# Key and value projections moved between the blocks of the recurrence, y carried through DRAM, and two pairs of 256-column projections done 512 columns at a time

## The chip, the cores and the metric

The kernel runs on one core of a Trainium2 chip. The metric is device microseconds from the first to the last instruction of that core. The engines that matter here are PE (TensorE, matmuls), DVE (VectorE), ACT (ScalarE), POOL (GpSimd) and SP, which issues all DMAs of this kernel from one queue, in its program's order.

## The reference

One decoder layer with T = 512 tokens and D = 1024 channels, in fp32. Two token mixers read the same normalized x: a gated linear recurrence over 1344 channels in 4 blocks, and sparse attention of 16 heads in 4 groups. Their outputs are merged by sigmoid gates, and a squared-ReLU MLP of width 4096 follows. The part that matters:

```python
xn = rmsnorm(x, norm_mix)
(u_rnn, u_gate, q, k_c, v_c, k_s, v_s, k_w, v_w, g_nsa, g_a, g_b) = jnp.split(xn @ w_in, cuts, axis=-1)
h_a = rg_lru(causal_depthwise_conv(u_rnn, conv_w, conv_b), gate_a_w, gate_a_b, gate_x_w, gate_x_b, lru_lambda)
y_a = h_a * jax.nn.gelu(u_gate, approximate=True)
y_b = nsa_mixer(q, k_c, v_c, k_s, v_s, k_w, v_w, g_nsa, rel_bias, ...)
merged = jax.nn.sigmoid(g_a) * (y_a @ proj_a) + jax.nn.sigmoid(g_b) * (y_b @ proj_b)
h = x + merged @ w_out
z = rmsnorm(h, norm_mlp) @ w_mlp_in
return h + jnp.square(jax.nn.relu(z)) @ w_mlp_out
```

`rg_lru` multiplies each block of 336 channels with two gate matrices and runs h[t] = a[t] h[t-1] + u[t] over the tokens. `k_s, v_s` and `k_w, v_w` are the keys and values (256 columns each) of the selected and of the window branch; `k_c, v_c` those of the compressed branch, which pass through a small MLP (phi) first.

## The kernel before

Every fp32 product is made of two parts. A weight tile `wraw` (2 buffers of 2048 elements a partition) comes by DMA; POOL rounds 1024 elements of it into `wh` (line 133) and DVE takes the rest into `wl` (line 134), each with 2 buffers. `mm3` (lines 138 to 140) then issues three matmuls: high by high, high by low, low by high. x is held as `XH` and `XL` in the same way, with channels on the partitions and 512 tokens behind them.

The work is written in this order. First x is normalized and transposed. Then `u_tiles` makes the column tiles of u, 128 columns each (tiles `mm`, 3 PSUM buffers, 24 matmuls of 512 tokens); `Cols` loads their weights in pairs and prepares the next tile's one ahead. Its sink puts the causal convolution into `uc`: one operation on ACT and three taps on DVE (line 326, 511, 510 and 509 elements), after which the PSUM buffer is free; or, for the tiles of the gate branch, gelu into `gg`. DMAs of SP repack `uc` into tiles `ub` of 112 channels for the blocks. `lru(b)` is one block of the recurrence: `ub` is split into `uh` and `ul`, 54 matmuls of 112 x 512 with the gate weights `gwh` and `gwl` follow (tiles `lru`, 4 PSUM buffers), and then a chain on ACT, POOL and DVE up to the scans on DVE (line 379). The result `rr` is repacked by DMAs into `hy`, and `y_tile(t)` multiplies it with `gg` on DVE and splits it at once into `YH` (POOL, line 390) and `YL` (DVE, line 391). The program's order is: tiles 0 to 5 of u, block 0, tiles 6 to 9, y, block 1, tiles 10 to 13, y, block 2, tiles 14 to 18, y, block 3, tiles 19 and 20, y.

Then come the token-major projections, `tok_cols`: KS, VS, KW (256 columns), VW (304, with the branch gates) and the queries of group 0 (256). The weights move and x stands still; four token tiles fill the four `lru` buffers, and a sink norms the heads of each (`head_norm`, tiles `sq` and `hrs`) or splits the values into `VV`. Then `ZW` makes the compressed keys and values as four column tiles like those of u (tiles `mm`, with their sinks `zdk` and `zdv`), phi follows, and with it, as filler of PE, the projection of y (`proj_a`, tiles `mf`, from `YH` and `YL`). In attention, a list of units of scores (tiles `sc`, line 850) and products with the values (`po`, line 888) is interleaved with more filler: the queries of groups 1 to 3 and the merge gates. `bias_copies` copies a row of the table of position biases to 128 partitions in DRAM, and `EC` takes nine small DMAs from a table.

Each engine runs its own instructions in a fixed order; the framework fixes it when the kernel is built, from a timeline that it works out, in which the splits of weights carry a raised priority of 300 (`PRIO`).

Of the kernel before, what the change touches and what calls it, by code (L numbers as in the profile page):

```python
# [68 lines left out]
def layer(ctx, tc, x, norm_mix, w_in, conv_w, conv_b, gate_a_w, gate_a_b, gate_x_w, gate_x_b,  # L69
# [22 lines left out]
    ya_es = ExitStack()  # L92
    yap = ya_es.enter_context(pool("ya", "right"))
    YH = yap.tile([128, NY, T], F32R, name="YH")
    YL = yap.tile([128, NY, T], F32R, name="YL")
    for t in (YH, YL):
        G.memset(f32(t[0:64, 0]), 0.0)
# [384 lines left out]
    kn = kv.tile([128, 4, 4, 2, 64], F32, name="kn")  # L482
    VV = kv.tile([128, 4, 2, 4, 128], F32R, name="VV")
    # the last token tile first
    gates = kv.tile([128, 4, 48], F32, name="gates")
    KC = kv.tile([128, 4, 2, 32], F32R, name="KC")
    QN = {0: kv.tile([128, 4, 256], F32, name="qn")}
    VC = kv.tile([128, 4, 2, 128], F32R, name="VC")
    G.memset(f32(VC), 0.0)

    def rstd_heads(sq, nh, name, pl):
        ss = pl.tile([128, nh], F32, name=name, bufs=2)
        V.tensor_reduce(ss, sq, axis=AX, op=OP.add)
        V.tensor_scalar(ss, ss, 1.0 / 64, EPS, op0=OP.mult, op1=OP.add)
        G.tensor_tensor(ss, ss, halfs[:, :nh], op=OP.pow)
        return ss
# [5 lines left out]
    # columns of w_in with the tokens on the partitions, four token tiles at once  # L502
    def tok_cols(c0, n, sink):
        step = WH // n
        pss = [psr.tile([128, T], F32, name="lru", bufs=4) for _ in range(4)]
        per = 8 if 8 * n <= WR else 4
        for k0 in [k for c in range(0, 8, per) for k in range(c, c + per, step)]:
            if k0 % per == 0:
                v = raw(128, per, n, (None, rows(win, c0, n)[:, k0:k0 + per]))
            kr = k0 % per  # L510
            k1 = min(kr + step, per) - kr + k0
            wh, wl = split(v[:, kr:kr + k1 - k0], k1 - k0, n)
            for i in range(4):
                ts = slice(128 * i, 128 * i + 128)
                for k in range(k0, k1):
                    mm3(pss[i][:, :n], XH[:, k, ts], XL[:, k, ts], wh[:, k - k0], wl[:, k - k0], k == 0, k == 7)
        for i in range(4):
            sink(i, pss[i])

    def head_norm(d4, ps, pl):  # L520
        sq = pl.tile([128, 4, 64], F32, name="sq", bufs=2)
        src = ps[:, :256].rearrange("p (h d) -> p h d", d=64)
        S.activation(d4, src, AF.Copy)
        S.activation(sq, src, AF.Square)
        rs = rstd_heads(sq, 4, "hrs", pl)
        V.tensor_tensor(d4, d4, rs.unsqueeze(2).to_broadcast([128, 4, 64]), op=OP.mult)

    def k_sink(br):
        def sink(i, ps):
            head_norm(kn[:, i, :, br], ps, kvp)  # L530
        return sink

    def v_sink(br):
        def sink(i, ps):
            src = ps[:, :256].rearrange("p (g d) -> p g d", d=64)
            S.activation(VV[:, i, br, :, 0:64], src, AF.Copy)
            V.tensor_tensor(VV[:, i, br, :, 64:128], src, f32(VV[:, i, br, :, 0:64]), op=OP.subtract)
            if br == 1:
                S.activation(gates[:, 3 - i], ps[:, 256:304], AF.Tanh, scale=0.5)
                V.tensor_scalar(gates[:, 3 - i], gates[:, 3 - i], 0.5, 0.5, op0=OP.mult, op1=OP.add)  # L540
                if i == 0:
                    gc = gates[:, 3].rearrange("p (h c) -> p h c", c=3)[:, :, 0]
                    # rows before the first whole block see no compressed key
                    G.affine_select(gc, gc, pattern=[[0, 16]], compare_op=OP.is_ge, fill=0.0,
                                    base=-31, channel_multiplier=1)
        return sink

    def q_sink(i, ps):
        head_norm(QN[0][:, i].rearrange("p (h d) -> p h d", d=64), ps, kvp)
# [59 lines left out]
    with pool("kvp") as kvp:  # L609
        tok_cols(COL_KS, 256, k_sink(0))  # L610
        tok_cols(COL_VS, 256, v_sink(0))
        tok_cols(COL_KW, 256, k_sink(1))
        tok_cols(COL_VW, 304, v_sink(1))
        for h in range(BC):
            bias_copies(h)
        tok_cols(COL_Q, 256, q_sink)
    with pool("ph") as ph:
# [569 lines left out]
```

## Time and profile before

| what | value |
|---|---|
| runs (median of 3) | 1084.92 us (1084.01 to 1088.92) |
| span of the profiled execution | 1088.0 us, mean granted clock 0.988 |
| PE busy | 1047.6 us (96%), 5405 matmuls |
| DVE busy | 669.0 us (61%) |
| POOL busy | 374.5 us (34%) |
| ACT busy | 348.1 us (32%) |
| DMA | 128.41 MB, mean 118 GB/s |

Shares of busy time are averages over the whole span. The time of the profiled execution is its span, 1088.0 us; it lies within the runs, at their upper end. "Granted clock" is the share of full speed at which TensorE was run; 1.00 is 2.4 GHz and 0.50 is 1.2 GHz.

### The profile page before, as it was taken

How to read it: one execution, taken by the hardware profiler on the slowest of the kernel's cores; microseconds unless marked ns; L12 is line 12 of the kernel's file. 1: busy time of each engine (PE TensorE's matmuls, PEld its weight loads, DVE VectorE, ACT ScalarE, POOL GpSimd, SP SyncE). 2: the span in 40 equal slices, each digit the busy share in tenths (PEclk: the TensorE clock that was granted, in tenths of full speed). 3: DMA queues.
4: the chain of work that ended last, by engine and by line, in shares of the span. 5: the costliest groups of instructions: out<-in, count | busy, mean ns of one | idle time of the engine just before them, and what ended most of it. 6: DMA issues, size and time to landing. Idle time of an engine off the chain costs nothing.

```text
span 1088.0 us, 14783 instructions
## 1 busy us (share of the span) xinstructions
PE 1047.6 (96%) x5405; PEld 885.4 (81%) x5405; DVE 669.0 (61%) x1225; ACT 348.1 (32%) x754; POOL 374.5 (34%) x411
## 2 busy tenths in 40 slices
PE   6999899999999999999999999899999999999998
PEld 5767677899778798988988877788888888888886
DVE  5589989954664597778778677554333334444443
ACT  4143353512332375756757611032111111111110
POOL 4243435444231274545646533201111121111110
PEclk9999899999999899999999999999999999999999
DMA  7635323433454633424333267521323233232322
GB/s 176 148 102 168 98 84 96 114 122 107 104 152 149 184 98 120 145 80 119 98 122 107 78 213 256 206 70 41 115 80 114 79 115 116 78 117 78 116 78 78
DMA packets 110199, 128.41 MB, mean 118 GB/s; under 512 B 23119, under 2 KB 87407, under 8 KB 110127
## 3 DMA queue, kind: packets, MB, share of 16 engines
q1 hardware_dynamic: 110127, 127.47, 38.9%
q8 instruction: 43, 0.70, 0.3%
q14 instruction: 29, 0.24, 0.1%
HBM read 109.45 MB, written 15.64 MB: 115 GB/s over the span
## 4 chain that ended last, share of the span: by engine, by line
PE 76%; DVE 9%; DMA 5%; issue 5%; POOL 2%; SPq 1%; ACT 1%; DVEq 0%; POOLq 0%; ACTq 0%
PE mf L138 5%; PE am L140 5%; PE am L139 5%; PE am L138 5%; PE mf L140 5%; PE mf L139 5%; PE mi L140 5%; PE mi L138 5%; PE mi L139 5%; PE sc L850 4%; PE po L888 4%; PE pt L869 3%; PE lru L139 2%; PE lru L140 2%; DVE wl L134 2%
## 5 line engine op out<-in xcount | busy, mean ns | idle before, releaser
L133 POOL TENSOR_SCALAR wh<-wraw 128x1024 fp32r<-128x1024 f32 (+2 forms) x115 | 127.0, 1108 | 260.9 <-PE mi L139 119.3
L134 DVE TENSOR_TENSOR wl<-wraw,wh 128x1024 fp32r<-128x1024 f32 (+2 forms) x115 | 141.7, 1235 | 42.0 <-POOL wh L133 37.5
L861 POOL TENSOR_SCALAR pp<-pp,sm,gates 128x512 f32<-128x512 f32 (+3 forms) x128 | 93.1, 735 | 71.3 <-DVE sm L859 58.4
L140 PE MATMUL am<-mwh,zl 128*128 128x512 f32 x256 | 99.3, 389 | 0.0
L139 PE MATMUL am<-mwl,zh 128*128 128x512 f32 x256 | 99.3, 389 | 0.0
L138 PE MATMUL am<-mwh,zh 128*128 128x512 f32 x256 | 98.8, 389 | 0.0
L140 PE MATMUL mi<-XH,wl 128*128 128x512 f32 x240 | 93.5, 390 | 0.3 <-DVE wl L134 0.3
L138 PE MATMUL mi<-XH,wh 128*128 128x512 f32 x240 | 93.4, 389 | 0.1
L139 PE MATMUL mi<-XL,wh 128*128 128x512 f32 x240 | 93.4, 389 | 0.0
L1130 DVE TENSOR_TENSOR zl<-Z,zh 128x512 fp32r<-128x512 f32 x32 | 36.3, 1136 | 88.4 <-ACT zh L1129 88.4
L140 PE MATMUL mm<-XH,wl 128*128 128x512 f32 (+1 forms) x216 | 83.5, 388 | 6.5 <-DVE wl L134 6.5
L138 PE MATMUL mm<-XH,wh 128*128 128x512 f32 (+1 forms) x216 | 83.4, 388 | 1.0 <-DVE uc L326 0.5
L139 PE MATMUL mm<-XL,wh 128*128 128x512 f32 (+1 forms) x216 | 83.0, 385 | 1.0 <-DVE XL L217 1.0
L133 POOL TENSOR_SCALAR mwh<-wraw 128x1024 fp32r<-128x1024 f32 x32 | 33.9, 1060 | 138.5 <-PE am L140 131.4
L1103 DVE SCALAR_TENSOR_TENSOR Z<-mi,zr 128x512 f32<-128x512 f32 x30 | 20.7, 691 | 97.3 <-ACT zr L1102 97.3
L858 ACT ACTIVATE pp<-pp,mx 128x512 f32<-128x512 f32 (+3 forms) x128 | 71.5, 560 | 27.9 <-DVE mx L856 24.8
L856 DVE CUSTOM_DVE_ANT_0 pp<-sc,BT 128x512 f32<-128x512 f32 (+3 forms) x128 | 59.1, 484 | 23.4 <-PE sc L850 11.0
L1129 ACT ACTIVATE zh<-Z 128x512 fp32r<-128x512 f32 x32 | 20.2, 632 | 136.5 <-PE am L139 134.4
L1102 ACT ACTIVATE zr<-mi 128x512 f32<-128x512 f32 x30 | 18.0, 600 | 141.7 <-PE mi L140 136.9
L875 ACT ACTIVATE PH<-pt 128x512 fp32r<-128x512 f32 (+1 forms) x96 | 49.2, 524 | 36.7 <-PE pt L869 35.9
L850 PE MATMUL sc<-KK,QS 128*128 128x512 f32 (+3 forms) x256 | 58.2, 334 | 2.5 <-DMA KK<-KK 2.5
L876 DVE TENSOR_TENSOR PL<-pt,PH 128x512 fp32r<-128x512 f32 (+1 forms) x96 | 55.8, 591 | 3.9 <-ACT PH L875 3.6
(258 smaller groups left out, 2683.6 us busy)
## 6 DMA issues: line engine op xcount, KB each, us to landing
wraw<-in_w_in_dram SPq DMA_DIRECT2D x26, 1024.0 KB, 5.4
wraw<-in_w_mlp_in_dram SPq DMA_DIRECT2D x16, 1024.0 KB, 5.5
wraw<-in_w_mlp_out_dram SPq DMA_DIRECT2D x16, 1024.0 KB, 4.8
tab_p<-tab_t SPq DMA_DIRECT2D x16, 320.0 KB, 5.4
wraw<-in_proj_a_dram SPq DMA_DIRECT2D x8, 640.0 KB, 6.1
BT<-tab_p SPq DMA_DIRECT2D x16, 256.0 KB, 3.5
wraw<-in_proj_b_dram SPq DMA_DIRECT2D x4, 1024.0 KB, 5.5
wraw<-in_w_out_dram SPq DMA_DIRECT2D x4, 1024.0 KB, 5.7
```

The source lines that it names most:

```text
L133: G.tensor_scalar(h, v, 1.0, 0.0, op0=OP.mult, op1=OP.add)
L134: V.tensor_tensor(l, v, f32(h), op=OP.subtract)
L138: PE.matmul(ps, lh, rh, start=start, stop=False)
L139: PE.matmul(ps, lh, rl, start=False, stop=False)
L140: PE.matmul(ps, ll, rh, start=False, stop=stop)
L850: ins = PE.matmul(ps[:, cs], grp.Q[r][:, ts], grp.K[br][:, hl, :128 * (i + 1)], start=hl == 0, stop=hl == 1)
L856: V.tensor_tensor_reduce(out=pp[:, cs], in0=ps[:, cs], in1=BTS[h][:, 384 - 128 * i:], scale=1.0, scalar=3e38, op0=OP.add, op1=OP.min, accu ...
L858: S.activation(pp[:, cs], pp[:, cs], AF.Exp, bias=mx, scale=-1.0, accum_out=sm)
L861: G.tensor_scalar(pp[:, cs], pp[:, cs], sm, gt, op0=OP.mult, op1=OP.mult)
L875: S.activation(ph, pv, AF.Copy)
L876: V.tensor_tensor(pl, pv, f32(ph), op=OP.subtract)
L888: PE.matmul(po[:, 128 * kt:], VV[:, kt, br, g], P[n][:, KT0[kt]:KT0[kt] + 128 * (4 - kt)], start=False, stop=br == 1 and kt == 3 and n == 1)
```

## The change

`tok_cols` moves up into the recurrence. KS and VS become one projection of 512 columns ahead of block 0; KW (256) comes ahead of block 1, behind tiles 6 to 9 of u; VW (304) ahead of block 2, behind tiles 10 to 13. The queries of groups 0 and 1 become one projection of 512 columns behind the recurrence, and the filler of group 1 in attention goes. Keys, values and queries get their memory before the recurrence; `YH` and `YL` get theirs after it. So `y_tile` writes y to DRAM (`y_d`), and `y_back` reads it (`yr`, 6 buffers) and splits it, two tiles ahead of the query projection and three in each of its steps. Every third column tile of u has buffers of its own for its split (`xwh`, `xwl`). `bias_copies` moves behind the queries.

```diff
         def prep(self, n, prio=PRIO):
             if n < len(self.starts) and n not in self.got:
-                self.got[n] = split(self.load(n), 8, 128, prio=prio)
+                own = {}
+                if self.third is not None and n % 3 == 2:
+                    own = {"pl": self.third, "tags": ("xwh", "xwl"), "bufs": 1}
+                self.got[n] = split(self.load(n), 8, 128, prio=prio, **own)
...
+    def s_sink(i, ps):
+        k_sink(0)(i, ps)
+        v_sink(0, 256)(i, ps)
+
+    def q_sink(i, ps):
+        for g in range(2):
+            head_norm(QN[g][:, i].rearrange("p (h d) -> p h d", d=64), ps, kvp, 256 * g)
...
         V.scalar_tensor_tensor(y, GG[t][p:], 0.5, y, op0=OP.mult, op1=OP.mult)
-        G.tensor_scalar(YH[p:, t], y, 1.0, 0.0, op0=OP.mult, op1=OP.add)
-        V.tensor_tensor(YL[p:, t], y, f32(YH[p:, t]), op=OP.subtract)
+        SP.dma_start(y_d[p:, t], y)
...
+    UW.third = rn
     for n in range(2):
         u_sink(UO[n])(p2[n])
     u_tiles(2, 2 + GT)
...
+    tok_cols(COL_KS, 512, s_sink)
     lru(0)
...
     u_tiles(6, 10)
+    tok_cols(COL_KW, 256, k_sink(1))
     for t in (1, 2):
         y_tile(t)
     lru(1)
     u_tiles(10, 14)
+    tok_cols(COL_VW, 304, v_sink(1))
...
+    def y_back(t):
+        p = 64 if t == 0 else 0
+        y = kvp.tile([128, T], F32, name="yr", bufs=6)[p:]
+        SP.dma_start(y, y_d[p:, t])
+        G.tensor_scalar(YH[p:, t], y, 1.0, 0.0, op0=OP.mult, op1=OP.add)
+        V.tensor_tensor(YL[p:, t], y, f32(YH[p:, t]), op=OP.subtract)
...
-    with pool("kvp") as kvp:
-        tok_cols(COL_KS, 256, k_sink(0))
-        tok_cols(COL_VS, 256, v_sink(0))
-        tok_cols(COL_KW, 256, k_sink(1))
-        tok_cols(COL_VW, 304, v_sink(1))
-        for h in range(BC):
-            bias_copies(h)
-        tok_cols(COL_Q, 256, q_sink)
+    back = iter([1, 2, 3, 4, 5, 6, 7, 8, 9, 10, 0])
+
+    def some_back(n):
+        for _, t in zip(range(n), back):
+            y_back(t)
+
+    with pool("kvq") as kvp:
+        some_back(2)
+        tok_cols(COL_Q, 512, q_sink, lambda: some_back(3))
+    for h in range(BC):
+        bias_copies(h)
...
-    work = 16 * 5.2 + 3 * 10.4 - TAIL
-    add_q(1)
+    work = 16 * 5.2 + 2 * 10.4 - TAIL
```

The order of DVE near the program's start, from behind the normalized rows of x to the fifth tile of u. Before (`uc_359` and `uc_367` are the first two tiles of u, out of PSUM tiles `mm_106` and `mm_107`, `uc_407` the third; `wl_375`, `wl_379` and `wl_422` are the weights of the third, fourth and fifth tile):

```order
L326 SCALAR_TENSOR_TENSOR uc_359<-mm_106,cw_310,uc_359 128x511
L134 TENSOR_TENSOR wl_375<-wraw_284,wh_374 128x1024
L326 SCALAR_TENSOR_TENSOR uc_359<-mm_106,cw_310,uc_359 128x510
L326 SCALAR_TENSOR_TENSOR uc_367<-mm_107,cw_310,uc_367 128x511
L134 TENSOR_TENSOR wl_379<-wraw_284,wh_378 128x1024
L326 SCALAR_TENSOR_TENSOR uc_359<-mm_106,cw_310,uc_359 128x509
L326 SCALAR_TENSOR_TENSOR uc_367<-mm_107,cw_310,uc_367 128x510
L326 SCALAR_TENSOR_TENSOR uc_367<-mm_107,cw_310,uc_367 128x509
L326 SCALAR_TENSOR_TENSOR uc_407<-mm_382,cw_310,uc_407 128x511
L134 TENSOR_TENSOR wl_422<-wraw_419,wh_421 128x1024
```


and now (`uc_364`, `uc_372` and `uc_412` are the same three tiles of u, `mm_99` and `mm_100` the PSUM tiles, `xwl_380`, `wl_384` and `wl_427` the weights of the third, fourth and fifth tile):

```order
L128 TENSOR_TENSOR xwl_380<-wraw_277,xwh_379 128x1024
L398 SCALAR_TENSOR_TENSOR uc_364<-mm_99,cw_303,uc_364 128x511
L128 TENSOR_TENSOR wl_384<-wraw_277,wh_383 128x1024
L398 SCALAR_TENSOR_TENSOR uc_364<-mm_99,cw_303,uc_364 128x510
L398 SCALAR_TENSOR_TENSOR uc_372<-mm_100,cw_303,uc_372 128x511
L128 TENSOR_TENSOR wl_427<-wraw_424,wh_426 128x1024
L398 SCALAR_TENSOR_TENSOR uc_364<-mm_99,cw_303,uc_364 128x509
L398 SCALAR_TENSOR_TENSOR uc_372<-mm_100,cw_303,uc_372 128x510
L398 SCALAR_TENSOR_TENSOR uc_372<-mm_100,cw_303,uc_372 128x509
L398 SCALAR_TENSOR_TENSOR uc_412<-mm_387,cw_303,uc_412 128x511
```


The weights of the fifth tile, `wl_427`, moved ahead of the last tap of the first tile (509 elements), the two last taps of the second and the first of the third.

The order of SP at the end of the recurrence. Before, from the repacking of the last block to the third key and value load behind it (`rr_1475` is the last block's result):

```order
L384 DMA hy_1572<-rr_1475 16x512
L384 DMA hy_1572<-rr_1475 112x512
L121 DMA wraw_1943<-in_w_in_dram 128x8x256
L480 DMA EC_1659<-tab_c_350 15x16x56
L480 DMA EC_1659<-tab_c_350 16x16x56 x7
L480 DMA EC_1659<-tab_c_350 1x16x56
L121 DMA wraw_2085<-in_w_in_dram 128x4x304
L121 DMA wraw_2143<-in_w_in_dram 128x4x304
```


and now, from the second of the three last writes of y, which follow the same repacking (`yr` are the reads, `wraw_2393` the weights of the third and fourth compressed column tile):

```order
L462 DMA y_d_349<-hy_2004 128x512
L462 DMA y_d_349<-hy_2009 128x512
L555 DMA EC_2093<-tab_c_343 15x16x56
L555 DMA EC_2093<-tab_c_343 16x16x56 x7
L555 DMA EC_2093<-tab_c_343 1x16x56
L571 DMA yr_2116<-y_d_349 128x512
L571 DMA yr_2120<-y_d_349 128x512
L571 DMA yr_2158<-y_d_349 128x512
L571 DMA yr_2162<-y_d_349 128x512
L571 DMA yr_2166<-y_d_349 128x512
L571 DMA yr_2198<-y_d_349 128x512
L115 DMA wraw_2393<-in_w_in_dram 128x8x256
```


The writes of y and its first six reads moved in, with the nine `EC` between them, ahead of `wraw_2393`; the loads of keys and values are gone from here.

The order of DVE behind the queries, up to the weights of the second compressed column tile. Before (`hrs` and `qn` belong to the norm of the queries, `wl_2377` are those weights):

```order
L493 TENSOR_REDUCE hrs_2342<-sq_2339 128x4
L494 TENSOR_SCALAR hrs_2342<-hrs_2342 128x4
L526 TENSOR_TENSOR qn_1673<-qn_1673,hrs_2334 128x256
L493 TENSOR_REDUCE hrs_2350<-sq_2347 128x4
L526 TENSOR_TENSOR qn_1673<-qn_1673,hrs_2342 128x256
L494 TENSOR_SCALAR hrs_2350<-hrs_2350 128x4
L493 TENSOR_REDUCE hrs_2358<-sq_2355 128x4
L134 TENSOR_TENSOR wl_2377<-wraw_2370,wh_2376 128x1024
```


and now (`wl_2361` are those weights, `YL_2110` is the low part of y, split from what was read back):

```order
L573 TENSOR_TENSOR YL_2110<-yr_2116,YH_2109 128x512
L339 TENSOR_TENSOR qn_356<-qn_356,hrs_2283 128x256
L309 TENSOR_REDUCE hrs_2299<-sq_2296 128x4
L339 TENSOR_TENSOR qn_357<-qn_357,hrs_2291 128x256
L310 TENSOR_SCALAR hrs_2299<-hrs_2299 128x4
L309 TENSOR_REDUCE hrs_2307<-sq_2304 128x4
L573 TENSOR_TENSOR YL_2110<-yr_2120,YH_2109 128x512
L310 TENSOR_SCALAR hrs_2307<-hrs_2307 128x4
L573 TENSOR_TENSOR YL_2110<-yr_2158,YH_2109 128x512
L128 TENSOR_TENSOR wl_2361<-wraw_2354,wh_2360 128x1024
```


Three splits of y, each of which needs a read of y, moved in ahead of the weights.

## Rows read from the trace of the kernel before

**Rows 1.** Windows of PE by stage: us, PE busy (instructions), clock, DMA share, GB/s.
```profile
29.80:54.50 24.70, 22.94 (x98) 1.00 0.67 164
54.50:194.30 139.80, 131.89 (x549) 0.98 0.39 113
194.30:290.70 96.40, 91.74 (x610) 0.98 0.42 116
290.70:380.00 89.30, 83.86 (x416) 0.96 0.50 148
```

**Rows 2.** Waits of PE in the recurrence: total us, times, longest us.
```profile
PE mm L140 <- DVE wl L134: 3.0, 1, 3.0
PE lru L140 <- DVE gwl L134: 2.5, 2, 1.3
```

**Rows 3.** Windows of PE: three idle stretches, each with the stretch behind it.
```profile
118.00:122.20 4.20, 1.06 (x4) 0.84 0.42 109
120.80:127.60 6.80, 5.37 (x13) 0.50 0.02 5
281.20:284.00 2.80, 0.50 (x3) 1.00 0.68 168
284.70:288.10 3.40, 3.40 (x10) 0.50 0.88 249
363.00:365.80 2.80, 0.36 (x2) 1.00 0.93 251
366.60:373.40 6.80, 6.80 (x22) 0.50 1.04 350
```

**Rows 4.** Windows of PE: 256-column matmuls alone, then 512-column matmuls alone.
```profile
210.00:237.00 27.00, 27.00 (x227) 1.00 0.50 143
1000.00:1050.00 50.00, 50.00 (x223) 1.00 0.25 85
```

**Rows 5.** Timeline of 28 to 50 us: start, duration, engine, line, operation [idle before].
```profile
32.88 2.18 DVE L326 SCALAR_TENSOR_TENSOR uc<-mm,cw,uc 128x509 f32<-128x509 f32 x3
...
33.01 1.60 SPq L121 DMA_DIRECT2D wraw<-in_w_in_dram  x2
...
35.67 0.39 PE L138 MATMUL mm<-XH,wh 128*128 128x512 f32 x1
...
39.25 1.05 POOL L133 TENSOR_SCALAR wh<-wraw 128x1024 fp32r<-128x1024 f32 x1 [7.82 <-DMA wraw<-in_w_in_dram]
...
40.34 1.23 DVE L134 TENSOR_TENSOR wl<-wraw,wh 128x1024 fp32r<-128x1024 f32 x1 [2.90 <-POOL wh L133]
...
41.48 0.74 DVE L326 SCALAR_TENSOR_TENSOR uc<-mm,cw,uc 128x510 f32<-128x510 f32 x1
```

**Rows 6.** Timeline: the last gate matmul of the recurrence.
```profile
194.05 0.40 PE L140 MATMUL lru<-uh,gwl 112*112 112x512 f32 x1
```

**Rows 7.** Timeline of 203 to 217 us: end of the recurrence.
```profile
204.21 3.44 DVE L379 TENSOR_TENSOR_SCAN rr<-ee,ii 112x512 f32<-112x512 f32 x3
...
209.83 6.80 SPq L480 DMA_DIRECT2D EC<-tab_c  x9
...
212.59 1.10 DVE L389 SCALAR_TENSOR_TENSOR hy<-gg,hy 128x512 f32<-128x512 f32 x1
```

**Rows 8.** The page's costliest groups: total busy us, mean ns of one.
```profile
L133 POOL TENSOR_SCALAR wh<-wraw 128x1024 fp32r<-128x1024 f32 (+2 forms) x115 | 127.0, 1108 | 260.9 <-PE mi L139 119.3
L134 DVE TENSOR_TENSOR wl<-wraw,wh 128x1024 fp32r<-128x1024 f32 (+2 forms) x115 | 141.7, 1235 | 42.0 <-POOL wh L133 37.5
L861 POOL TENSOR_SCALAR pp<-pp,sm,gates 128x512 f32<-128x512 f32 (+3 forms) x128 | 93.1, 735 | 71.3 <-DVE sm L859 58.4
```

**Rows 9.** Groups of POOL and DVE by line: the splits of y.
```profile
L390 POOL TENSOR_SCALAR YH<-hy 128x512 fp32r<-128x512 f32 (+1 forms) x11 | 13.3, 1207 | 17.0 <-DVE hy L389 16.9
L391 DVE TENSOR_TENSOR YL<-hy,YH 128x512 fp32r<-128x512 f32 (+1 forms) x11 | 10.2, 937 | 1.1 <-POOL YH L390 1.0
```

**Rows 10.** DMA issues by tile: count, KB each, us to landing.
```profile
pp<-yb_d SPq DMA_DIRECT2D x7, 256.0 KB, 3.1
```

More of the change, by code (lines that the diff above doesn't have):

```diff
@@ L91, in layer @@
     XL = xtp.tile([128, 8, T], F32R, name="XL")
[L92 to L97, printed above, removed]
     psr_es = ExitStack()
@@ L148, in __init__ @@
         def __init__(self, w, starts):
-            self.w, self.starts, self.got, self.raws = w, starts, {}, {}
+            self.w, self.starts, self.got, self.raws, self.third = w, starts, {}, {}, None
         def load(self, n, pair=True):
@@ L287, in layer @@
     spill = {n: dram.tile([128, 8, T], F32, name="sp_" + n) for n in ("ta", "tb", "pa")}
+    y_d = dram.tile([128, NY, T], F32, name="y_d")
     def spill_sink(n, m):
@@ L297, in spill_sink, with rstd_heads @@
         return sink
+    kv_es = ExitStack()
+    kv = kv_es.enter_context(pool("kv"))
+    kn = kv.tile([128, 4, 4, 2, 64], F32, name="kn")
+    VV = kv.tile([128, 4, 2, 4, 128], F32R, name="VV")
+    gates = kv.tile([128, 4, 48], F32, name="gates")
+    QN = {g: kv.tile([128, 4, 256], F32, name="qn", bufs=2) for g in range(2)}
+    kvp_es = ExitStack()
+    kvp = kvp_es.enter_context(pool("kvp"))
+    def rstd_heads(sq, nh, name, pl):
+        ss = pl.tile([128, nh], F32, name=name, bufs=2)
+        V.tensor_reduce(ss, sq, axis=AX, op=OP.add)
+        V.tensor_scalar(ss, ss, 1.0 / 64, EPS, op0=OP.mult, op1=OP.add)
+        G.tensor_tensor(ss, ss, halfs[:, :nh], op=OP.pow)
+        return ss
@@ new lines, in tok_cols @@
+    def tok_cols(c0, n, sink, aside=lambda: None):
+        step = WH // n
+        pss = [psr.tile([128, T], F32, name="lru", bufs=4) for _ in range(4)]
+        per = 8 if 8 * n <= WR else 4
+        for k0 in [k for c in range(0, 8, per) for k in range(c, c + per, step)]:
+            if k0 % per == 0:
+                v = raw(128, per, n, (None, rows(win, c0, n)[:, k0:k0 + per]))
+            kr = k0 % per
+            k1 = min(kr + step, per) - kr + k0
+            wh, wl = split(v[:, kr:kr + k1 - k0], k1 - k0, n)
+            for i in range(4):
+                ts = slice(128 * i, 128 * i + 128)
+                for k in range(k0, k1):
+                    mm3(pss[i][:, :n], XH[:, k, ts], XL[:, k, ts], wh[:, k - k0], wl[:, k - k0], k == 0, k == 7)
+            aside()
+        for i in range(4):
+            sink(i, pss[i])
@@ L469, in layer @@
     rn_es.close()
-    kv_es = ExitStack()
-    kv = kv_es.enter_context(pool("kv"))
-    EC = kv.tile([128, 16, 56], F32, name="EC")
+    kvp_es.close()
+    kv2 = kv_es.enter_context(pool("kv2"))
+    EC = kv2.tile([128, 16, 56], F32, name="EC")
     for a in range(9):
@@ L480, in layer @@
         SP.dma_start(EC[p0:p0 + b1 - b0], src)
[L482 to L488, printed above, removed]
-    G.memset(f32(VC), 0.0)
[L491 to L496, printed above, removed]
+    KC = kv2.tile([128, 4, 2, 32], F32R, name="KC")
+    VC = kv2.tile([128, 4, 2, 128], F32R, name="VC")
+    G.memset(f32(VC), 0.0)
+    ya_es = ExitStack()
+    yap = ya_es.enter_context(pool("ya", "right"))
+    YH = yap.tile([128, NY, T], F32R, name="YH")
+    YL = yap.tile([128, NY, T], F32R, name="YL")
+    for t in (YH, YL):
+        G.memset(f32(t[0:64, 0]), 0.0)
+    def y_back(t):
[4 more added lines that the diff above has]
+        V.tensor_tensor(YL[p:, t], y, f32(YH[p:, t]), op=OP.subtract)
     def bias_copies(h):
@@ L500, in bias_copies @@
             tc.keep_in_program_order(SP.dma_start(tab_p[h], tab_t[h:h + 1].to_broadcast([128, 640])))
[L503 to L549, printed above, removed]
     def pa_gen():
@@ L723, in q_gen @@
     def q_gen(g):
-        QN[g] = kv.tile([128, 4, 256], F32, name="qn")
+        QN[g] = kv.tile([128, 4, 256], F32, name="qn", bufs=2)
         for i in range(4):
@@ L953, in layer @@
                         if ev == "q0":
-                            while (g + 1, 3) not in QN:
+                            while g > 0 and (g + 1, 3) not in QN:
                                 fill.pump(0.1)
```

24 lines of the change are left out of this document (added).

## The prediction

> **What bounds the kernel now.** The page's table of busy times, read first, has TensorE (PE) busy for 1047.6 of 1088.0 us, so this is a matmul kernel and a change can win in two ways only: cheaper matmuls, or less time in which PE stands. PE's windows by stage show where it stands [rows 1]: 24.70 − 22.94 = 1.8 us while the first columns of u are made, 139.80 − 131.89 = 7.9 us in the recurrence, 4.7 us in the token-major projections and the compressed columns behind them, 5.4 us up to the first scores. The change touches just these four stretches. PE's waits in the recurrence are named next, and they end with DVE, which makes there the low parts of the weights between its scans [rows 2]. A stand also costs something after it. Behind idle stretches of 3.1, 2.3 and 2.4 us the granted clock is 0.50, the lower level of 1.2 GHz, for 6.8, 3.4 and 6.8 us [rows 3]; PE works at half rate in its busy time there (5.4, 3.4 and 6.8 us), which costs 2.7, 1.7 and 3.4 us more. With that the recurrence loses 7.9 + 2.7 = 10.6 us, the token-major stage 4.7 + 1.7 = 6.4.
>
> The span (1088.0) lies 3.1 us above the median of the runs (1084.92) and 0.9 below the highest (1088.92). I work out a difference from this trace and put it on the median.
>
> **Merged columns.** KS with VS, and Q of groups 0 and 1, become 512 columns wide: 2 pairs x 8 k-tiles x 4 token tiles x 3 = 192 matmuls of 512 columns take the place of 384 of 256. In a stretch of only 256-column matmuls 227 take 27.00 us, 0.119 each; 223 of 512 columns take 50.00 us, 0.224 each [rows 4]. A pair saves 0.238 − 0.224 = 0.014 us, 192 pairs 2.6: **−2.6 us**. Bounds: 0 and no more than this. The Trainium skill ("TensorE: Matmul & The Clock Gate", Back-to-back issue gap) gives columns / 2.4 + 2.5 ns between two warm matmuls taken alone, so a merge would save 2.5 ns a pair, by that rule 0.5 us in all. The rows differ from it, and the sum goes by the rows.
>
> **The third weight buffer moves a split ahead of a release.** This is my largest term. Before, DVE finished the three taps of uc for the first tile (the last of them, of 509 elements, in the group at 32.88) long before the weights of the fifth tile of u came: SP issued their load at 33.01, POOL split them at 39.25, DVE at 40.34 [rows 5]. Weights and taps share DVE's queue, and the wait of 2.90 us at 40.34 held the tap that ran at 41.48. In the new order the wl of that load stands ahead of the 509-element tap of the first PSUM tile. The SP order up to there is unchanged, so I take 39.25 for POOL and 40.34 for DVE again; the tap is then done at 41.48 + 0.74 = 42.2. The fourth tile of u takes the first tile's PSUM buffer (there are three), and PE came to it at 35.67. So PE stands 42.2 − 35.7 = 6.5 us: **+6.5**. The 1.8 us of waits that this stretch had go, since xwh and xwl have their own buffer and stand ahead of the splits of the recurrence's input: **−1.8**. Behind so long a stand I expect half clock for 3.4 to 6.8 us [rows 3], which costs 1.7 to 3.4: **+2.5**. The stand is shorter only if the weights land sooner; with the longest half clock the three come to +8.1, and to +1.8 less if the old waits stay.
>
> **Keys and values inside the recurrence.** KS and VS bring 96 matmuls of 512 columns, KW 96 of 256, VW 96 of 304: 21.5 + 11.4 + 13.6 = 46 us of PE work that needs nothing from the recurrence, just where PE stands. But each 1024 elements of weights need a wh (1.11 us on POOL) and a wl (1.24 on DVE) [rows 8], ten of each here, in the same queues as the scans. In the new order the second wl of KW comes behind the scans of block 0 and its hy products, the second load of VW behind two y writes on SP, and one tile of u waits for the gg of an earlier one on DVE. Each of these is about one queued operation late, between a scan (3.44 / 3 = 1.15 us [rows 7]) and the rest of a load (33.01 to 39.25, 6.2 us [rows 5]): I put them at 1.5, 3.8 and 1.7, KS at 0.3, together 7.3 us, and none long enough to bring down the clock. Against the 10.6 of before that is −3.3. Bounds: 0 (new waits as long as the old) and −10.6 (all gaps filled). The 11 splits of y leave DVE and POOL here, 0.94 and 1.21 us each [rows 9], which is what the ten new splits bring; with the same work on both queues spread over 46 us more, I go past the listing, to **−5.0**.
>
> **y through DRAM: hidden in the recurrence, late at its end.** 11 writes and 11 reads at some 0.8 us of SP each (two loads in 1.60 [rows 5]) lie beside PE's work for blocks 0 to 2. At the end they don't. Count from t0 = 194.3, when the last gate matmul has run [rows 6]. The scans ended 13.4 us after it (204.21 + 3.44), the last product of y 19.4 after it (212.59 + 1.10) [rows 7]. After the change PE has only 11 matmuls of u there (2.5 us) and then Q, 4 steps of 24 matmuls of 0.224 = 5.4 us. Its third step would start at t0 + 13.3; its wl stands behind the scans, 13.4 + 1.2 = 14.6, a wait of 1.3. Then come the compressed columns: the first tile ends at 2.5 + 21.5 + 1.3 + 5.4 = t0 + 30.7. The wl of the second stands on DVE behind three YL, and those wait for y to come back: product 19.4, one more write 0.8, nine EC in 6.80 [rows 7], three reads 2.4, a landing of 3.1 as for yb_d [rows 10], then 1.21 on POOL, 0.94 and 1.24 on DVE: t0 + 35.9, a wait of 5.2. What is late next is the first split of proj_a, whose buffer comes free only with the end of the third tile: 1.11 + 1.24 = 2.3. Together 8.8, and 1.7 of half clock: 10.5 against 6.4, **+4.1**. Bounds: −2 (the read-back is covered by Q, and the two other waits of 3.6 and 0.8 of clock are left) and +8 (the rival below, less its later clock).
>
> **The start of attention.** The last tile of proj_a (33 matmuls, 7.4 us) now stands ahead of the first scores and covers the idle 2.4 us at 363 [rows 3]. But then six score tiles follow with no filler between them. POOL takes 0.74 us for a tile [rows 8], two matmuls 0.45, so PE waits 6 x 0.29 = 1.7 and one passage through three engines, an estimate of 3 x 0.74 = 2.2. 3.9 − 2.4 = **+1.5**. Bounds: −5.8 (the stand and its half clock are gone, nothing comes) and +3.9.
>
> The later bias copies and memsets cost PE nothing: POOL is busy for 374.5 us of 1088, and the tables' copies are read only in attention; without that cover they would cost what the reads of y do, 0.8 us of SP each.
>
> **Sum.** −2.6 + 6.5 − 1.8 + 2.5 − 5.0 + 4.1 + 1.5 = +5.2; 1084.9 + 5.2 = **1090.1 us**.
>
> **Rivals.** *The gaps close* (the other side). The recurrence gains its full 10.6, Q covers the read-back, and attention starts at no cost: −2.6 + 7.2 − 10.6 + 0 + 0 = −6.0, so 1078.9. It decides if no wait of the recurrence is longer than a split, 1.2 us. For it: 46 us of independent work, and the only releaser is DVE [rows 2]; against it: PE takes its work in the order written, and the new weights come through the queue that is late. *The early stand is paid back.* While PE stands, DVE, POOL and the loads get ahead by 6 us, and as much of the later waits vanishes: 1090.1 − 6 = 1084.1. Against it: with two buffers a split can't run further ahead than PE's release of the last one. *The read-back holds the weights.* The second pair of compressed columns is loaded behind nine EC and six reads: 19.4 + 0.8 + 6.8 + 4.8 + 6.2 + 2.3 = t0 + 40.3, and PE wants it at 30.7 + 5.2 + 5.4 = 41.3. One us more and it is the wait; if the reads go one at a time, 3.1 each, it is 6 x 2.3 = 14 us later, the first proj_a with it, of which some 10 are left when the 5.2 grow too: 1099. *The page's rule* for the merge, told above: 2.1 us more, 1092.2.
>
> **Chances.** A measurement of this kernel can tell 0.5% (5.4 us) from no change. My sum 0.45: 0.23 within 0.5% and 0.22 above, since it lies 0.2 us below that bound. Gaps close 0.25 (faster). Paid back 0.12 (same). Reads hold weights 0.13 and the page's rule 0.05 (slower). So faster 0.25, same 0.35, slower 0.40. The range 1076 to 1099 leaves out the far half of the two outer cases.
>
> **What would show it.** Right: PE idle from about 35.5 to 42 and released by a tap of uc, granted clock 0.50 behind it; short waits for wl behind scans in the recurrence; a wait of some 5 us for wl in the compressed columns, and YL waiting for y there. Wrong: no stand near 35 us, over 10 us of waits in the recurrence, or compressed columns without a gap. The price of the early stand hangs on one number, the 39.25 at which the weights can be split; the tail's on whether the reads of y start as soon as SP comes to them.

## The result, and the profile after

The changed kernel's median is 1098.83 us in its first four runs, against 1084.57 for the kernel before; the ratio of the two is 1.0111, with a 95% interval of 1.0082 to 1.0140. A second set of six runs gives 1100.29 and a ratio of 1.0105 (1.0083 to 1.0128). So it is slower by about 1%, 12 us by the mean spans and 14 by the medians. The first median lies 0.2 us inside the upper end of the range (1076 to 1099), the second 1.3 above it, and the first is 9 us above the forecast of 1090.1.

PE's windows by stage, of the changed kernel, answer to [rows 1]: first columns of u, recurrence with keys and values, queries and compressed columns, phi, then attention.

```profile
30.20:60.50 30.30, 24.07 (x98) 0.89 0.64 170
60.50:250.50 190.00, 182.61 (x859) 0.98 0.39 116
250.50:304.00 53.50, 46.34 (x194) 0.97 0.50 152
304.00:391.50 87.50, 81.55 (x401) 1.00 0.53 149
391.50:652.00 260.50, 256.61 (x1590) 1.00 0.41 123
```

Idle in the first four is 6.2, 7.4, 7.2 and 6.0 us, where before it was 1.8, 7.9, 4.7 and 5.4. The recurrence's window has 50.7 us more of PE work in it, 46 of it the projections, and PE stands there almost as long as before. In attention 3.9 us of idle lie where the same stretch of the kernel before had 260.93 busy of 261.00. Of these, 2.5 lie between 391.5 and 420, right behind the first scores; a wait of 0.6 near 651 isn't new, since the kernel before has it too, just outside its window.

The early stand, in the timeline of 30 to 46 us (to be held against [rows 5]):

```profile
32.04 1.25 SPq L115 DMA_DIRECT2D wraw<-in_w_in_dram  x2
...
38.10 1.04 POOL L127 TENSOR_SCALAR wh<-wraw 128x1024 fp32r<-128x1024 f32 x1 [8.92 <-DMA wraw<-in_w_in_dram]
...
39.18 2.05 DVE L128 TENSOR_TENSOR wl<-wraw,wh 128x1024 fp32r<-128x1024 f32 x1 [6.96 <-POOL wh L127]
...
41.15 2.83 DVE L398 SCALAR_TENSOR_TENSOR uc<-mm,cw,uc 128x509 f32<-128x509 f32 x4
...
42.03 0.76 PE L132 MATMUL mm<-XH,wh 128*128 128x512 f32 x1 [6.24 <-DVE uc L398]
```

It reads from the top down: the load is issued, POOL waits 8.92 us for it, DVE 6.96 for POOL, and behind that wl stands the 509-element tap that releases PE after 6.24 us.

The granted clock behind three stands, in windows of PE (the first line is the first stand itself), answers to [rows 3]:

```profile
35.80:42.00 6.20, 0.00 (x0) 0.83 0.71 235
39.80:46.60 6.80, 4.57 (x11) 0.50 0.32 91
...
231.00:237.80 6.80, 5.21 (x12) 0.50 0.77 225
...
299.30:302.70 3.40, 3.19 (x8) 0.50 1.00 278
```

The waits of PE in the recurrence, from 50 to 225 us (total us, times, longest), answer to [rows 2]:

```profile
PE lru L132 <- POOL wh L127: 1.7, 1, 1.7
PE lru L133 <- DVE wl L128: 1.2, 2, 0.7
PE lru L133 <- DVE ul L426: 1.2, 1, 1.2
```

the same at the recurrence's end and in the compressed columns, 225 to 300 us:

```profile
PE mf L132 <- POOL wh L127: 4.2, 1, 4.2
PE mm L132 <- DVE gg L389: 3.3, 1, 3.3
PE mm L134 <- DVE wl L128: 2.8, 2, 2.3
```

and from there to the first units of attention, 300 to 420 us:

```profile
PE mf L132 <- POOL wh L127: 2.7, 4, 1.0
PE sc L882 <- DMA KK<-KK: 2.1, 1, 2.1
PE mf L134 <- DVE wl L128: 1.2, 4, 0.3
PE pt L847 <- POOL scc L840: 1.1, 1, 1.1
```

The read-back of y, in the timeline from 264 to 300 us:

```profile
264.92 2.46 SPq L462 DMA_DIRECT2D y_d<-hy  x3
...
267.42 4.44 SPq L555 DMA_DIRECT2D EC<-tab_c  x9
...
271.91 3.39 SPq L571 DMA_DIRECT2D yr<-y_d  x6
...
281.45 1.62 DVE L128 TENSOR_TENSOR wl<-wraw,wh 128x1024 fp32r<-128x1024 f32 x1
...
283.13 0.50 PE L134 MATMUL mm<-XH,wl 128*128 128x512 f32 x1 [2.25 <-DVE wl L128]
...
293.32 0.85 POOL L572 TENSOR_SCALAR YH<-yr 64x512 fp32r<-64x512 f32 x1
...
295.27 2.76 POOL L311 TENSOR_TENSOR hrs<-hrs,halfs 128x4 f32<-128x4 f32 x2
...
298.02 0.82 POOL L127 TENSOR_SCALAR wh<-wraw 128x768 fp32r<-128x768 f32 x1
...
298.89 0.50 PE L132 MATMUL mf<-YH,wh 128*128 128x512 f32 x1 [4.16 <-POOL wh L127]
```

SP goes through the writes, EC and the reads in turn, and wl comes out behind them. The wh of 298.02, the first of proj_a, stands at the end of POOL's queue: from 285.88 POOL hardly pauses, with five YH (4.7 us), four `hrs` norms of the queries (5.4 us) and two other wh ahead of it. The norms of group 1's queries are among that work only because the two groups were merged.

**Two parts of the time.** Each run lists its span and its mean granted clock. Span x clock is roughly the time that the run would have taken at full clock; the rest is roughly what the lower level cost. It is only roughly that, since the mean clock counts idle time too: of the 20.4 us at 0.50 in the changed kernel's trace, PE is busy for 16.4. Over 56 runs of the kernel before, spans go from 1079.8 to 1089.7 us with a standard deviation of 1.9 us, and span x clock has one of 1.3. For the changed kernel the two sets of runs differ by 3.0 us in this product (1083.9 and 1080.9), so a difference of 2 us between two kernels says little. The comparisons below give both parts (means over the runs of a kernel):

| kernel | runs | span, us | mean clock | span x clock | the rest |
|---|---|---|---|---|---|
| before | 56 | 1084.9 | 0.9915 | 1075.6 | 9.3 |
| changed (both sets) | 10 | 1097.1 | 0.9863 | 1082.1 | 15.0 |
| no third buffer | 6 | 1095.7 | 0.9855 | 1079.8 | 15.9 |
| third buffer from tile 8 | 5 | 1096.0 | 0.9850 | 1079.5 | 16.4 |
| both merges alone | 12 | 1088.4 | 0.9873 | 1074.6 | 13.8 |
| KS and VS merged alone | 12 | 1084.7 | 0.9913 | 1075.3 | 9.4 |
| y through DRAM alone | 6 | 1091.5 | 0.9878 | 1078.2 | 13.3 |
| early stand filled | 4 | 1099.5 | 0.9860 | 1084.1 | 15.4 |
| keys and values back | 6 | 1092.1 | 0.9870 | 1077.9 | 14.2 |
| EC early | 6 | 1096.1 | 0.9848 | 1079.5 | 16.6 |
| EC early, q1 filler | 6 | 1095.4 | 0.9857 | 1079.7 | 15.7 |
| YH on ACT | 6 | 1094.1 | 0.9855 | 1078.3 | 15.9 |
| keys and values back, YH on ACT | 6 | 1092.6 | 0.9867 | 1078.1 | 14.6 |

Of the 12.2 us between the kernels, 6.4 are in span x clock and 5.8 in the rest.

### The profile page after: what moved, and what is told of

The parts are those of the page before. It is cut to its first block, busy times and chain, and to the rows that moved or that the text cites. A ratio compares the mean times of both kernels' runs of the same rounds, so it can differ in the third digit from the quotient of the medians.

```text
span 1094.6 us, 14420 instructions
## 1 busy us (share of the span) xinstructions
PE 1043.3 (95%) x5213; PEld 873.7 (80%) x5213; DVE 670.2 (61%) x1225; ACT 349.0 (32%) x754; POOL 372.5 (34%) x411
## 4 chain that ended last, share of the span: by engine, by line
PE 73%; DVE 10%; issue 6%; DMA 6%; POOL 3%; ACT 1%; SPq 1%; POOLq 0%; DVEq 0%; ACTq 0%
PE am L134 5%; PE am L133 5%; PE am L132 5%; PE mi L134 5%; PE mi L132 5%; PE mi L133 5%; PE mf L132 5%; PE mf L134 5%; PE mf L133 5%; PE po L920 4%; PE sc L882 3%; PE pt L901 3%; DMA wraw<-in_w_in_dram 2%; DVE wl L128 2%; PE lru L133 2%
## 5 line engine op out<-in xcount | busy, mean ns | idle before, releaser
L127 POOL TENSOR_SCALAR wh<-wraw 128x1024 fp32r<-128x1024 f32 (+2 forms) x108 | 116.9, 1086 | 284.1 <-PE mi L133 119.1
L128 DVE TENSOR_TENSOR wl<-wraw,wh 128x1024 fp32r<-128x1024 f32 (+2 forms) x108 | 133.2, 1238 | 40.6 <-POOL wh L127 34.5
L132 PE MATMUL mm<-XH,wh 128*128 128x512 f32 (+1 forms) x160 | 62.1, 390 | 9.5 <-DVE uc L398 6.2
L134 PE MATMUL mm<-XH,wl 128*128 128x512 f32 (+1 forms) x160 | 61.3, 384 | 2.8 <-DVE wl L128 2.8
L133 PE MATMUL mm<-XL,wh 128*128 128x512 f32 (+1 forms) x160 | 61.5, 386 | 1.0 <-DVE XL L214 1.0
```

Source lines behind the costliest of these rows:

```text
L127: G.tensor_scalar(h, v, 1.0, 0.0, op0=OP.mult, op1=OP.add)
L128: V.tensor_tensor(l, v, f32(h), op=OP.subtract)
L132: PE.matmul(ps, lh, rh, start=start, stop=False)
L133: PE.matmul(ps, lh, rl, start=False, stop=False)
L134: PE.matmul(ps, ll, rh, start=False, stop=stop)
```

## The experiments

**The third buffer.** Two runs, on the changed kernel:

```diff
-    UW.third = rn
```

> The changed kernel without the third split buffer (one line, UW.third = rn, taken out). DVE's order at the start is then that of the kernel before. Theory (the early stand is a cost of its own): the 6.4 us stand of TensorE at 35.4 us goes, with it the half clock behind it (6.8 us in the trace of the changed kernel, 2.3 of them idle, so some 2.2), and the waits of 1.8 us near 47 come back: about 7 us faster than the changed kernel, 1091 to 1093 against its 1098.8. Rival (paid back): the time comes back as later waits, 1097 to 1099.

```diff
-            if self.third is not None and n % 3 == 2:
+            if self.third is not None and n % 3 == 2 and n > 5:
```

> The changed kernel with the third split buffer used only from column tile 8 on. Theory: no early stand either, and the cover of the later splits is kept, so 1091 to 1093, within 1 us of the run without any third buffer. Rival (the third buffer is what fills the recurrence's gaps): 3 us or more faster than the run without it, 1088 to 1090.

Without it: 1098.69, ratio to before 1.0102 (1.0081 to 1.0123). From tile 8 on: 1097.85, 1.0105 (1.0086 to 1.0123). The early stand is gone in both, and the time is the same within a microsecond or two, where the theory had 1091 to 1093: the rival "paid back" has it. PE's waits without the third buffer, first from 28 to 60 us, then from 60 to 250:

```profile
PE mm L134 <- DVE wl L128: 3.4, 3, 2.3
PE mm L132 <- POOL wh L127: 0.5, 1, 0.5
...
PE mm L134 <- DVE wl L128: 4.2, 2, 3.3
PE mm L132 <- DVE uc L398: 1.7, 1, 1.7
PE lru L132 <- POOL uh L425: 1.7, 1, 1.7
PE lru L133 <- DVE ul L426: 0.4, 1, 0.4
```

3.9 us of waits stand where the one of 6.2 was, and the recurrence waits for wl (3.3) where the changed kernel doesn't. In span x clock it is 2.3 us better than the changed kernel, less than the changed kernel's two sets differ, at 0.9 us more of the rest. The second run isn't 3 us better than the first, so the buffer isn't what fills the recurrence's gaps either.

**The merges alone**, on the kernel before: KS and VS in one call of 512 columns, and the queries of groups 0 and 1 likewise, in their old place; group 1's filler goes.

```diff
-        tok_cols(COL_KS, 256, k_sink(0))
-        tok_cols(COL_VS, 256, v_sink(0))
+        tok_cols(COL_KS, 512, s_sink)
...
-        tok_cols(COL_Q, 256, q_sink)
+        tok_cols(COL_Q, 512, q_sink)
...
-    add_q(1)
```

> The kernel before with the two merges alone: KS with VS, and the queries of groups 0 and 1, 512 columns wide, in their old place behind the recurrence; group 1's queries are no longer filler. Theory (rows of pitch): 2.6 us faster than before, 1082.0. By the Trainium skill's rule of 2.5 ns a pair 0.5 us faster, 1084. Rival (the filler is missed in attention): 2 us or more slower, 1087 or above, with idle TensorE between the score tiles.

1090.0, ratio 1.0035 (1.0019 to 1.0050): slower, as the rival has it. The waits of PE from 420 to 460 us, where the kernel before has none:

```profile
PE sc L854 <- DMA KK<-KK: 4.2, 1, 4.2
```

The first scores of group 1 wait for its keys, where queries of group 1 were filler before. In span x clock the kernel is still 1.0 us better than before, but it has 4.5 us more of the rest.

```diff
-        tok_cols(COL_KS, 256, k_sink(0))
-        tok_cols(COL_VS, 256, v_sink(0))
+        tok_cols(COL_KS, 512, s_sink)
```

> The kernel before with KS and VS merged to 512 columns in their old place, and nothing else; the queries of group 1 stay filler. Theory (the merge is worth its pitch, and the loss of the run with both merges came from the queries of group 1): 96 pairs at 0.014 us, 1.3 us faster than before in span times clock, the 4.2 us wait for KK near 435 us gone, within 0.3% of before in time. Rival (the merge itself costs, by longer steps between weights): 2 us or more slower, waits in the KS and VS stretch.

With KS and VS alone: 1086.31 against 1086.82, ratio 0.9992 (0.9977 to 1.0008), and no such wait. So the loss came from the queries. What 96 pairs are worth can't be told from the runs: span x clock differs by 0.3 us with a scatter of 1. The traces can tell it. PE from the first matmul of KS to the last of KW, in the kernel before and then in this one:

```profile
201.57:237.89 36.32, 34.86 (x289) 1.00 0.43 123
...
203.16:238.11 34.95, 33.59 (x194) 1.00 0.48 128
```

The same products take 34.86 us of PE apart and 33.59 merged: 1.27 us for 96 pairs, as the rows of pitch had it. By the Trainium skill ("TensorE: Matmul & The Clock Gate", Back-to-back issue gap) it would be an estimated 0.2 us, from 2.5 ns a pair; the trace does not agree.

**y through DRAM alone**, on the kernel before: `y_tile` writes, and `y_back` reads during KS and VS.

```diff
+        some_back(2)
-        tok_cols(COL_KS, 256, k_sink(0))
-        tok_cols(COL_VS, 256, v_sink(0))
+        tok_cols(COL_KS, 256, k_sink(0), lambda: some_back(3))
+        tok_cols(COL_VS, 256, v_sink(0), lambda: some_back(3))
```

> The kernel before with y through DRAM alone: written tile by tile, read back and split during the KS and VS projections, two tiles ahead and three in each step; nothing else moved. Theory (the round trip is hidden where TensorE has work that does not need DVE's next split at once, and costs where a weight split stands behind it): a wait of 3 to 6 us for a wl or a raw tile near 215 to 235 us, 1088 to 1091. Rival (hidden, as in the blocks before): within 1 us of before, 1084 to 1086.

1093.32, ratio 1.0064 (1.0041 to 1.0086). The wait is where it was expected, in the timeline of 222 to 234 us:

```profile
223.18 3.71 SPq L502 DMA_DIRECT2D yr<-y_d  x5
...
228.09 0.80 PE L132 MATMUL lru<-wh,XH 128*128 128x256 f32 x2 [3.21 <-POOL wh L127]
...
230.18 0.58 PE L133 MATMUL lru<-wl,XH 128*128 128x256 f32 x1 [1.29 <-DVE wl L128]
```

The whole costs 6.6 us of span, 2.6 of it in span x clock and 4.0 in the rest, a little more than expected.

**The early stand filled.** 27 matmuls behind the third tile of u read x and write a PSUM tile that nobody reads:

```diff
     u_tiles(2, 2 + GT)
+    pw = psr.tile([128, T], F32, name="lru", bufs=4)
+    for _ in range(27):
+        tc.keep_in_program_order(PE.matmul(pw, XH[:, 0, 0:128], XH[:, 0], start=True, stop=True))
```

> The changed kernel with 27 matmuls of 512 columns put on TensorE between the third and the fourth tile of u, where it stands for 6.4 us. They read x, write a PSUM tile of their own that nobody reads, and fill that time alone. Theory (the clock is part of the price): nothing ends earlier by them, but the granted clock stays at 1.00 behind the stand, where it was 0.50 for 6.8 us with 4.5 of them busy: 2 us faster than the changed kernel, about 1096.5, and the half clock near 40 us gone from the trace. Rival (the clock falls later instead, or the stand alone counts): no half clock near 40 but the same time, 1098 to 1100.

1100.88, ratio 1.0135 (1.0115 to 1.0154), in four runs: not faster. Windows of PE over the filled stand, what follows it, and a later stretch:

```profile
35.30:41.50 6.20, 6.01 (x27) 1.00 0.97 323
41.50:48.00 6.50, 4.96 (x22) 1.00 0.36 100
57.00:62.00 5.00, 2.90 (x13) 1.00 0.00 2
62.50:69.30 6.80, 5.64 (x13) 0.50 0.17 39
```

The clock behind the stand is 1.00, as the theory has it, and it is 0.50 from 62.5 on instead, behind a stretch with 2.1 us of idle. The time isn't better, so the rival holds. This kernel has a new wait there (2.1 us for wh of KS), which the changed kernel hasn't, so what the clock alone was worth stays open.

**Keys and values moved back**, on the kernel without the third buffer: KS and VS (512), KW and VW stand behind block 3, ahead of the queries; y still goes through DRAM.

```diff
-    tok_cols(COL_KS, 512, s_sink)
     lru(0)
...
-    tok_cols(COL_KW, 256, k_sink(1))
...
-    tok_cols(COL_VW, 304, v_sink(1))
...
+    tok_cols(COL_KS, 512, s_sink)
+    tok_cols(COL_KW, 256, k_sink(1))
+    tok_cols(COL_VW, 304, v_sink(1))
     kvp_es.close()
```

> The changed kernel without the third buffer, and with KS and VS (512), KW and VW moved back behind the recurrence, ahead of the queries; y still goes through DRAM and is read back in the queries. Theory (the projections inside the recurrence fill little, since their own weights wait behind the scans; their absence leaves the read-back without cover): the recurrence's waits stay within 2 us of the run without the third buffer, the waits of the compressed columns go because 46 us of projections lie ahead of them: 4 to 8 us faster than that run, 1091 to 1095. Rival (they do fill the recurrence): its waits grow by 4 us or more, 1097 to 1101.

1094.26, ratio 1.0067 (1.0049 to 1.0084), against 1098.69 with them inside: 4.4 us faster, as the theory has it. Its waits from 60 to 250 us:

```profile
PE mm L134 <- DVE wl L128: 4.1, 2, 3.2
PE lru L132 <- POOL YH L571: 4.1, 1, 4.1
PE lru L134 <- DVE gwl L128: 1.1, 1, 1.1
PE mm L132 <- POOL wh L127: 1.0, 1, 1.0
PE lru L132 <- POOL uh L425: 0.7, 1, 0.7
PE lru L133 <- DVE ul L426: 0.3, 1, 0.3
```

With the 4.1 us of waits that it has from 28 to 60 us and without the read-back (YH, 4.1), that is 11.3 us; with the projections inside the recurrence the same two stretches have 11.9. So in these two traces they fill nothing there. One wait of the read-back stays, in KS. And the wait of 4.2 us for KK near 440 us, known from the merges alone, is in this trace too; with the projections inside, no trace has a wait of that size there.

**EC moved**, on the kernel without the third buffer: the loop over EC goes behind `lru(1)`.

> The changed kernel without the third buffer, and with the nine EC transfers issued behind block 1 instead of ahead of the reads of y (EC gets its memory ahead of the recurrence). Theory (SP's queue holds the read-back): the reads start 4.4 us earlier (nine EC took 4.44 us of SP), so the waits of 4.2 and 1.3 us in the compressed columns shrink by 3 to 4 us: 1094 to 1096 against 1098.7 without the third buffer alone. Rival (the y products and the normed queries on DVE and POOL set it): waits unchanged within 1 us, 1098 to 1100.

1098.09, ratio 1.0104 (1.0087 to 1.0120): as without. The run tells nothing of SP's queue, though. In the kernel that it was built on, the nine EC stand at 142.56 us already, since its order came out another way than the changed kernel's; they moved to 107, both far ahead of the reads. The comparison that tells is that kernel against the changed one: EC away from the reads, the reads start at once behind the last write, and the waits there are 1.1, 4.0, 0.9 and 0.8 us instead of 2.3, 0.5 and 4.2. So with EC away the waits add up to about as much, 6.8 us against 7.0, though much else in the order differs too.

**EC moved, and group 1's queries as filler again** (`tok_cols(COL_Q, 256, ...)`, `add_q(1)`).

> The kernel of the EC run, and with the queries of group 0 alone (256 columns) behind the recurrence and those of group 1 as filler in attention again. Theory: attention's first waits (2.3, 0.8, 1.3 us in the trace of the changed kernel) shrink by 3 us and their half clock with them, but 10.8 us of queries less cover the read-back, which then shows: 1095 to 1100, no gain over the EC run. Rival (the read-back is no longer late once EC is away): 1090 to 1093.

1096.68, ratio 1.0099 (1.0079 to 1.0120), and no gain over the EC run in span x clock: the theory. Attention's waits between the score tiles go, and the compressed columns and proj_a behind them have waits of 3.4, 2.0 and 2.1 us, as the theory has it for less PE work over the read-back.

**The changed kernel again.**

> The changed kernel unchanged, once more, so that it and the kernel before lie in one set of runs. Theory (its loss is some 8 us of waits at full clock and some 4 us of lower clock): 1097 to 1099, mean granted clock about 0.988 against 0.992 of before. Rival (the first runs were a chance of the clock): 1091 to 1094.

1100.29, ratio 1.0105; mean clock 0.985 against 0.991. The loss is no chance of the first runs. Its two parts were 8.2 and 3.4 by the first four runs and are 6.4 and 5.8 over all ten. The second trace shows where the clock differs. PE idles as long as in the first (29.7 us in the five stretches of the first table against 30.6), but the span is 4.0 us longer at a clock of 0.984 against 0.991, and among the stretches at 0.50 are some that the first trace has at full clock. One stands behind the wait for KK, 2.4 us long here and 2.1 in the first trace, where the clock behind it was 1.00:

```profile
397.30:404.10 6.80, 6.80 (x26) 0.51 0.81 286
```

**YH made on ACT**, on the kernel without the third buffer and on the one with keys and values back:

```diff
-        G.tensor_scalar(YH[p:, t], y, 1.0, 0.0, op0=OP.mult, op1=OP.add)
+        S.activation(YH[p:, t], y, AF.Copy)
```

> The changed kernel without the third buffer, and with the high part of the y that is read back made on ScalarE instead of GpSimd. Theory (GpSimd's queue holds the compressed columns: the wh of the second pair stands behind five YH, which wait for the reads, and behind the queries' norms): the 4.0 us wait of the third tile for wh falls below 1.5 us, and the time by 2 to 4 us: 1095 to 1097. Rival (the loads or DVE's YL hold it as much): a wait of 3 us or more at the same place, named by a load or by wl, 1098 to 1100.

> The kernel with the keys and values moved back behind the recurrence (y through DRAM, no third buffer), and with that high part made on ScalarE. Theory: the one wait of 4.1 us that was named by GpSimd's YH in the KS and VS stretch goes: 1090 to 1092. Rival (the read-back is late whoever splits it, since the reads wait for the last products of y): a wait of 3 us or more stays there, 1093 to 1095.

The first: 1096.16, ratio 1.0081 (1.0058 to 1.0104), span x clock 1.5 us better than its base, with a scatter of 2 in six runs each. The 4.0 us wait for wh in the compressed columns is 0.2, so it was POOL's queue; half of it comes back one step on, at the first weights of proj_a (2.6 us, 0.8 in the base). Waits of PE from 200 to 310 us:

```profile
PE mf L132 <- POOL wh L127: 2.6, 1, 2.6
PE mm L134 <- DVE wl L128: 1.9, 1, 1.9
...
PE mm L132 <- POOL wh L127: 0.2, 1, 0.2
```

The second: 1094.0, ratio 1.0071 (1.0051 to 1.0090), no faster than its base, in the rival's range. Its wait of 4.1 is one of 2.5, now for the norms:

```profile
PE lru L132 <- DVE hrs L310: 2.5, 1, 2.5
```

No version here beats the kernel before.

## Why the prediction came out as it did

The experiments build a chain from the kernel before to the changed one, in mean spans: the merges 1084.9 to 1088.4 (+3.5), y through DRAM on top of them 1092.1 (+3.7), the keys and values moved inside 1095.7 (+3.5), the third buffer 1097.1 (+1.5). The steps were run in different sets, in which the kernel before lies between 1084.5 and 1085.4, and small parts of the order move with them, as EC does in the run without the third buffer. The sum had −2.6, +4.1, −5.0 and +7.2 for these, and +1.5 for the start of attention. So only y through DRAM came out as booked. That the forecast pointed the right way is luck: without the early stand it would have been 2.0 us faster. That the first median lies inside the range is luck too, since the upper end came from the rival with the reads one at a time, and six reads took 3.39 us of SP, with no wait of the third compressed tile for its wh.

**Merged columns (−2.6).** The price of a pair was right: 1.27 us for 96 pairs in the traces, so 2.5 for 192, and the rival by the Trainium skill's rule is wrong here. In span x clock the two merges alone give −1.0 with a scatter of about 1.4 in each run, and in span +3.5. What the sum left out is that a query projection taken from attention leaves its place empty: 4.2 us of wait in the merges alone. The changed kernel doesn't have that wait (from 420 to 500 PE is busy for 80.00 of 80.00 us); what keeps it away there is open. It has the norms of the second group ahead of proj_a instead.

**The early stand (+6.5, −1.8, +2.5).** The mechanism was right to 0.3 us: idle from 35.8 to 42.0, released by the tap behind wl, half clock for 6.8 us with 4.57 busy, so 2.3 lost; the old 1.8 us of waits went too. But as a term of the sum it was wrong. Taking it away brought 1.5 us of span and nothing in the median. The trace without the stand shows waits that come back at wl, 3.9 us in all up to 60 us and one of 3.3 in the recurrence. So for this term the rival "paid back" came nearest; its mechanism, that the other engines get ahead while PE stands, fits these waits but no run shows it apart. The time that the rival gave, 1084, was far off, since the rest did not follow.

**Keys and values inside the recurrence (−5.0).** This is the step that failed by most. The stage's idle went from 7.9 to 7.4 us, and moving the projections back made the kernel 4.4 us faster by the median (3.5 in span). With what the half clock behind the gg wait costs (6.8 us with 5.21 busy, so 2.6) the stage loses 10.0 against 10.6 before: a gain of 0.6 where 5.0 was booked. The listing of new waits (7.3 us) was near the stage's idle of 7.4, and roughly so place by place: the split behind the scans 0.7 (KW, 1.5 expected), VW 1.7 and 0.5 (3.8), the gg 3.3 (1.7), and 1.2 for ul that was not expected. What went wrong was to go past the listing to −5.0, and to book 2.7 us of clock as gained: the 6.8 us at 0.50 are still there, behind the gg wait of 3.3 us. The gaps-close rival rested on DVE as the only releaser; its rows leave out a wait of 1.6 us for POOL's uh in the same stretch of before, and here POOL's wh holds PE for 1.7. The reason given for going further, that DVE's and POOL's work is spread over 46 us more, would need the projections' own weights to be ready when PE stands; their waits show that they were not.

**y through DRAM (+4.1).** Right in its place and about in its size. Expected were waits of 1.3 in the queries, 5.2 in the second compressed tile and 2.3 at proj_a; the trace has none, 2.3 (and 0.5 for another wl) and 4.2. The stage's idle is 7.2 us against 4.7, and y through DRAM alone costs 6.6 us of span. With the half clock behind the last wait (3.19 us busy, 1.6 lost) the stage loses 8.8 against 6.4, +2.4. EC took 4.44 us of SP and not 6.80. The wait at proj_a came another way than in the sum: not the buffer but POOL's queue held it, with YH and the norms of the queries, and POOL's queue shows in the run with YH on ACT too (4.0 us became 0.2, and half of that came back one step on).

**The start of attention (+1.5).** KK's wait was not covered: 2.1 us of it are left (2.5 before), and why its transfer still came late is open. What the start costs hangs on the clock. Up to 420 us it is 8.4 us of idle in the first trace, at a clock of 1.00; before it was 5.4 of idle and 3.4 of half clock, 8.8 together. In the second trace 6.5 us of idle and two stretches at 0.50 (3.4 and 6.8 us, both busy throughout) make 11.6. So the term came out between −0.4 and +2.8.

**The clock.** The sum booked +2.5, −2.7 and about 0 for the tail, nothing in all. The runs have 5.8 us more of it. And the trace of before, on which the sum was made, is the slowest of its runs (1088.92 of 1084.01 to 1088.92), at a clock of 0.988 against a mean of 0.9915. A difference against it undersells a loss: the profiled executions differ by 7.4 us, the medians by 14.

## What to carry to other kernels

Work put between the blocks of a chain fills PE's waits only if its own operands don't come through the queue that PE waits for; here each projection's weights went through DVE and POOL behind the scans. A long wait in the trace is not its price: take it away in a run of its own before it is called a cost, since waits further on can take its place. Work taken out of a later stretch leaves a gap there that has to be priced too. Compare kernels by span x clock and the rest apart, over several runs, before a few microseconds are explained.

## What the runs showed of the hardware

The runs of one kernel differ by up to 10 us, and much of it goes with the granted clock: the kernel before has 1079.8 us at 0.995 and 1089.7 at 0.987, and the products are 1074.4 and 1075.5. It is not all of it, since span x clock still scatters by 1.3 us there and by 2.2 in the changed kernel. The rest, which goes with the clock, is 9.4 to 16.6 us in the other kernels and 9.3 in the kernel before. Filling one stand with matmuls kept the clock at 1.00 behind it and found it at 0.50 20 us on. Two executions of the changed kernel with nearly the same stands have 0.50 behind different ones. What decides behind which stand it falls is open.
